# Attention pairs beside the head group of their own number, the last group in a written order, and a gate's modulation summed at the front

## The chip, the cores and the metric

The kernel runs on one core of a Trainium2 chip, in one launch. The metric is device microseconds. The core's engines are TensorE (PE; its weight loads are PEld), VectorE (DVE), ScalarE (ACT), GpSimd (POOL) and SyncE (SP), which here only issues transfers. Each engine works through its own instructions in order and waits on semaphores for the others. A trace's profiled execution is one run of its own.

## The reference

A backbone of two layers works on 512 latent tokens x and 256 context tokens, 1024 wide, in float32; the output is the latent stream.

```python
for i in range(DEPTH):
    mx = jnp.split((cond_x @ ada_w[i] + ada_b[i])[:, None, :], 6, axis=-1)
    mc = jnp.split((cond_c @ ada_w[i] + ada_b[i])[None, None, :], 6, axis=-1)
    ux = modulate(hx, mx[0], mx[1])
    uc = modulate(hc, mc[0], mc[1])
    if i % 2 == 0:
        ox, oc = hybrid_mixer(ux, uc, ...)
    else:
        ox, oc = diff_mixer(ux, uc, ...)
    hx = layer_norm(ALPHA * hx + mx[2] * ox, ln1_g[i], ln1_b[i])
    fx = conv_ffn(modulate(hx, mx[3], mx[4]), ...)
    hx = layer_norm(ALPHA * hx + mx[5] * fx, ln2_g[i], ln2_b[i])
    if not last:
        # the same for hc with mc
```

Layer 0 is the hybrid. One input projection gives z, xbc, dt, q, k and v. The SSD branch (16 heads in 4 groups) works in chunks of 128 tokens: states per chunk, a scan over them in both directions, `y_diag = (C B^T * decay) x` and `y_off = C prev`, then `y * silu(z)` and an RMS norm. Beside it stand 8 heads of neighbourhood attention, whose softmax takes a window of the grid and all context keys; the context attends to itself. `concat(y, a) @ w_out` ends the mixer. Layer 1 has differential attention. Each layer has an FFN with a convolution over three tokens. `mx[5]`, `mc[5]` of layer 0, the gate of its FFN, is called (0, 5) here, or the second gate.

## The kernel before

Matrix products are done in three passes: weights and activations are split into a high half (`whi`, a rounded copy made on ACT) and a low half (`wlo`, the difference, made on DVE or POOL in `wchunk`, L152 to L176), and `PASS` multiplies high by high, high by low and low by high. Tokens lie in six tiles of 128, four of x and two of the context.

The modulation needs a product of the two condition vectors with 1024 x 6144 weights per layer. `ada_steps` (L190) does it on PE. `ada_dve` (L208) does it on DVE: it loads 512 KB at a time (`araw`, two slots under the tag `ar`, shared with `grow` and `yr`), adds up each row times the condition's value in `acc` (L221, L223; for two conditions 32 instructions of 128x512 for one of the six vectors), and lets PE sum over partitions (`adaps`, L229). These pieces are a background list, of which the FFN takes steps.

The hybrid layer, until about 675 us, has at the front the first modulations and the modulated input, the projections of group 0 (`dense_ssd`, `dense_z`, `x_rows`), and then four SSD groups. `ssd_group(g)` transposes B (`btp`), makes the five states (`xw` on POOL, `Sps` on PE, the scan `PV` on POOL and DVE), and then takes six chunks: load the decay rows (`E`, a transfer on POOL's queue from `scr`), eight exponentials on ACT, four pairs of products on DVE (L684, L685), `gp` = B C^T on PE and its product with the decay (L688), `op` = C times the state before it (L695, `t` at L697), `gp` again for the product with x (L706), then the gate with silu(z). `na_pair(p)` splits q and k of a head pair into halves (`split_qk`, `nQ` at L750, `nKh`, `nKl`), transposes V (`vtp`), and takes six units of 128 queries: scores `S` on PE, bias, maximum `nm`, exponential and normalised `P` on DVE and ACT (L799 to L802), transposes of P on PE and their copy `Pt`, and the product with V.

`run` takes a step of the group and of a pair in turn and a step of a list of filler at each second turn; the framework then sets the order of instructions on every engine by a simulated timeline and a priority. While `pe.chain` is True, every matmul through `pe` is tied behind the one before it in the written order. Group g runs beside pair g-1, with the projections of group g+1 and of pair g as filler. In group 3, the filler is pair 3's projection and `early`: it transposes the gated y (`ytp`) and starts two banks of `w_out` (`po`, with 18 matmuls for the six first of eight rows of 128). Pair 3 comes after the group: gate rows `G` are loaded and summed (L291), q and k are split, and its units stand in turn with a `piece` of `w_out`. Then come the other banks, their evacuation (`ev` on DVE, the addition to y on POOL), the last two rows (`out_y2`), the attention's part (`out_att`) and the layer norm.

In the FFN of layer 0, `up(j)` makes two projections (`fpx` for x, `fpc` for the context), with the convolution `cv` on ACT and DVE (L1077, L1081). POOL makes the low half of chunks 4 to 9 (`W_POOL`), and the layer norm's `affine` (L409, `y<-y,gb` on POOL) is tied behind the first of these. `STEPS0` takes five background steps after each of the two up-projections of the second pair, and the first two pieces are the second gate (0, 5) itself.

Of the kernel before, what the change touches and what calls it, by code (L numbers as in the profile page):

```python
# [46 lines left out]
STEPS0 = 5  # L47

ADA_LATER = 100

W_POOL = ((4, 5, 6, 7, 8, 9), (4, 6, 8))
# [23 lines left out]
def emit(tc, T):  # L75
# [74 lines left out]
    pool_wlo = [None]  # L150

    def wchunk(src, shape, gate=None, eng=None, rows=None, rp=None):  # L152
# [55 lines left out]
    def ada_dve(l, w, h, accp, pool, pstag, **atag):  # L208
# [18 lines left out]
        for s in range(ns):  # L227
            for j in range(4):
                nc.tensor.matmul(ps[32 * j:32 * j + 32, 128 * s:128 * s + 128], ones[:, 0:32], acc[:, s, 128 * j:128 * j + 128],  # L229
                                 start=True, stop=True)  # L230
# [52 lines left out]
    def gate_rows(l, which, s, pool, tag, bufs=None, scaled=True):  # L283
# [4 lines left out]
        G = pool.tile([128, D], F32, name="G", tag=tag, bufs=bufs)  # L288
# [50 lines left out]
    def tc_mm(ps, w, u, tt):  # L339
        n = len(PASS) * KC  # L340
        i = 0
        for kc in range(KC):
            for wi, ui in PASS:
                nc.tensor.matmul(ps, u_dst(u, kc, ui, tt), w(kc, wi), start=(i == 0), stop=(i == n - 1))  # L344
                i += 1
# [249 lines left out]
    def dense_z(g):  # L595
        w = by_kc(wrows(T["w_z"][g], 2, (4, 256)), 4)
        for t2 in range(3):
            pz = pmm.tile([128, 2, 256], F32, name="pz", tag="mm")
            zt = sp.tile([128, 2, 256], F32, name="zs", tag="zs", bufs=3)
            for i in range(2):  # L600
                tc_mm(pz[:, i], w, u, 2 * t2 + i)
            nc.scalar.activation(zt, pz, AF.Silu)
# [19 lines left out]
    def ssd_group(g, BC, xs):  # L622
# [37 lines left out]
        for k in range(5):  # L660
# [4 lines left out]
            nc.tensor.matmul(p[:, 0], Bt[:, FO[k]], xw[FO[k]][:, 0].rearrange("p h q -> p (h q)"), start=True, stop=True)  # L665
            nc.tensor.matmul(p[:, 1], Bt[:, BO[k]], xw[BO[k]][:, 1].rearrange("p h q -> p (h q)"), start=True, stop=True)
# [7 lines left out]
        for c in (4, 5, 0, 1, 2, 3):  # L674
# [891 lines left out]
```

## Time and profile before

| | |
|---|---|
| median of 3 runs | 2028.44 us (2028.31 to 2029.06) |
| profiled execution | 2025.07 us, of which the span is 2023.3 |
| mean granted clock of PE | 0.978 |
| PE busy | 1920.8 us, 95% of the span |
| DVE, ACT, POOL busy | 1352.1, 920.5, 769.6 us |
| moved by DMA | 217.59 MB, mean 108 GB/s |

The span runs from the first instruction to the last one. A busy PE may be a slow PE: the granted clock is shown beside it, 1.00 for 2.4 GHz and 0.50 for 1.2 GHz. Waits name the instruction that ended them by line and tile.

### The profile page before, as it was taken

To read this page: it belongs to the slowest core of one execution; us is meant where nothing else is said; L and a number is where in the kernel's file an instruction comes from. 1 tells how busy PE (TensorE), PEld (TensorE's weight loads), DVE (VectorE), ACT (ScalarE), POOL (GpSimd) and SP (SyncE) were. 2 spreads that over 40 slices of the span, in tenths; PEclk is the share of its full clock that TensorE was granted. 3 is DMA by queue.
4 is the path that set the end of the run, shared out by engine and by line. 5 is a ranking of instruction groups with operands and counts; after the bars stand their busy time and mean duration, and the time that the engine had idled before them with its cause. 6 is when DMAs were issued, how large, how long until landed. Compare 5 with 4: busy or idle time off the path is not lost.

```text
span 2023.3 us, 31146 instructions
## 1 busy us (share of the span) xinstructions
PE 1920.8 (95%) x11928; PEld 1645.3 (81%) x11928; DVE 1352.1 (67%) x2172; ACT 920.5 (45%) x1799; POOL 769.6 (38%) x658
## 2 busy tenths in 40 slices
PE   7998999998699889999999999899999899999997
PEld 5887889887477788878888888899998788888886
DVE  3757565765556887887676667566665876655566
ACT  3545466585442732323222234656665644333332
POOL 2135224336315675444444408431115264222133
PEclk9999999999699989999999999999999999999999
DMA  9335342233422243433343342222122223323321
GB/s 314 113 114 170 110 129 76 96 117 117 155 68 88 87 135 100 130 116 115 105 144 106 104 135 86 92 73 85 55 66 68 89 64 126 104 84 104 103 96 62
DMA packets 109445, 217.59 MB, mean 108 GB/s; under 512 B 27112, under 2 KB 45904, under 8 KB 109296
## 3 DMA queue, kind: packets, MB, share of 16 engines
q1 hardware_dynamic: 95168, 187.87, 28.9%
q0 software_dynamic: 6016, 20.03, 2.8%
q10 hardware_dynamic: 8112, 7.71, 1.3%
q8 instruction: 94, 1.54, 0.3%
q14 instruction: 55, 0.45, 0.1%
HBM read 202.81 MB, written 8.55 MB: 104 GB/s over the span
## 4 chain that ended last, share of the span: by engine, by line
PE 72%; DVE 12%; DMA 4%; POOL 4%; ACT 4%; issue 3%; ACTq 0%; SPq 0%; DVEq 0%; POOLq 0%
PE fpx L328 20%; PE pdn L1122 11%; PE px L328 7%; PE fpc L328 5%; PE S L108 3%; PE po L108 3%; PE pc L328 3%; PE pz L344 3%; DVE acc L223 2%; PE pv L344 2%; DMA araw<-in_ada_w 2%; POOL y L409 2%; PE dSp L1329 2%; PE po L1005 2%; PE pk L328 2%
## 5 line engine op out<-in xcount | busy, mean ns | idle before, releaser
L172 ACT ACTIVATE whi<-raw 128x1024 fp32r<-128x1024 f32 (+1 forms) x203 | 213.4, 1056 | 443.5 <-PE fpc L328 167.2
L173 DVE TENSOR_TENSOR wlo<-raw,whi 128x1024 fp32r<-128x1024 f32 (+1 forms) x190 | 251.8, 1330 | 157.4 <-ACT whi L172 144.6
L352 POOL TENSOR_TENSOR y<-y,ev 128x512 f32<-128x512 f32 x144 | 212.5, 1495 | 185.1 <-DVE ev L350 175.2
L1122 PE MATMUL pdn<-whi,fact 128*128 128x512 f32 x880 | 273.1, 392 | 2.1 <-DVE ev L350 1.8
L328 PE MATMUL fpx<-ux,whi 128*128 128x512 f32 (+1 forms) x832 | 232.3, 363 | 8.2 <-DVE cv L1081 7.6
L328 PE MATMUL fpx<-u,whi 128*128 128x512 f32 (+1 forms) x832 | 226.5, 358 | 2.4 <-DVE cv L1081 1.5
L1122 PEld LDWEIGHTS pdn<-whi,fact 128*128 128x128 f32 x880 | 162.4, 188 | 37.2 <-DVE ev L350 2.9
L328 PEld LDWEIGHTS fpx<-ux,whi 128*128 128x128 f32 x832 | 150.3, 194 | 31.1 <-ACT whi L172 8.0
L1122 PE MATMUL pdn<-wlo,fact 128*128 128x512 f32 x440 | 170.8, 390 | 0.7 <-DVE wlo L173 0.7
L328 PEld LDWEIGHTS fpx<-u,whi 128*128 128x128 f32 x832 | 149.2, 191 | 25.1 <-ACT cv L1077 1.6
L328 PE MATMUL fpx<-ux,wlo 128*128 128x512 f32 (+1 forms) x416 | 151.1, 364 | 8.5 <-POOL wlo L173 6.6
L223 DVE SCALAR_TENSOR_TENSOR acc<-araw,condp,acc 128x512 f32<-128x512 f32 x140 | 137.4, 1002 | 24.4 <-DMA araw<-in_ada_w 24.0
L1106 POOL TENSOR_TENSOR fact<-cv,fact 128x768 fp32r<-128x768 f32 (+1 forms) x44 | 70.6, 1605 | 217.5 <-ACT fact L1105 217.5
L328 PE MATMUL fpx<-u,wlo 128*128 128x512 f32 (+1 forms) x416 | 148.8, 358 | 1.1 <-DVE wlo L173 1.1
L328 PE MATMUL px<-ux,whi 128*128 128x512 f32 x448 | 148.5, 405 | 0.0
L171 POOL TENSOR_TENSOR raw<-raw,G 128x1024 f32<-128x1024 f32 x30 | 74.4, 2482 | 193.0 <-DMA raw<-in_w_down 113.0
L1081 DVE SCALAR_TENSOR_TENSOR cv<-fpx,fcw,cv 128x511 f32<-128x511 f32 x176 | 130.3, 744 | 20.8 <-ACT cv L1077 19.6
L328 PE MATMUL fpc<-uc,whi 128*128 128x256 f32 x704 | 130.2, 283 | 0.0
L328 PEld LDWEIGHTS fpc<-uc,whi 128*128 128x128 f32 x704 | 112.6, 191 | 4.2 <-issue 0.6
L409 POOL TENSOR_TENSOR y<-y,gb 128x256 f32<-128x256 f32 x112 | 98.9, 918 | 35.2 <-PE lntp L388 28.7
L1077 ACT ACTIVATE cv<-fpx,fcw 128x512 f32<-128x512 f32 x88 | 67.8, 771 | 80.7 <-PE fpx L328 76.5
L350 DVE SCALAR_TENSOR_TENSOR ev<-pdn,G 128x512 f32<-128x512 f32 x120 | 81.3, 683 | 32.0 <-POOL y L352 18.9
(335 smaller groups left out, 4628.0 us busy)
## 6 DMA issues: line engine op xcount, KB each, us to landing
araw<-in_ada_w SPq DMA_DIRECT2D x96, 512.0 KB
raw<-in_w_up SPq DMA_DIRECT2D x88, 512.0 KB
raw<-in_w_down SPq DMA_DIRECT2D x44, 512.0 KB
E<-scr POOLq DMA_DIRECT2D x24, 512.0 KB, 5.4
raw<-in_w_dqk SPq DMA_DIRECT2D x16, 512.0 KB
raw<-in_w_qkv SPq DMA_DIRECT2D x12, 512.0 KB
raw<-in_w_out SPq DMA_DIRECT2D x12, 512.0 KB
raw<-in_w_bc SPq DMA_DIRECT2D x8, 512.0 KB
```

The costliest lines, as they stand in the source:

```text
L108: i = f(*a, **k)
L171: nc.gpsimd.tensor_tensor(raw, raw, gate, op=OP.mult)
L172: nc.scalar.activation(hi[:, :n], raw[:, :n], AF.Copy)
L173: i = (eng or nc.vector).tensor_tensor(lo[:, :n], raw[:, :n], hi[:, :n].bitcast(F32), op=OP.subtract)
L223: nc.vector.scalar_tensor_tensor(acc[:, s], raw[:, i], cs, acc[:, s], op0=OP.mult, op1=OP.add)
L328: nc.tensor.matmul(ps, w[wi][:, kc], rhs(kc, ui), start=(i == 0), stop=(i == n - 1))
L344: nc.tensor.matmul(ps, u_dst(u, kc, ui, tt), w(kc, wi), start=(i == 0), stop=(i == n - 1))
L350: nc.vector.scalar_tensor_tensor(t, ps, r, Gh, op0=OP.mult, op1=OP.mult)
L352: eng.tensor_tensor(yh, yh, t, op=OP.add)
L409: i = nc.gpsimd.tensor_tensor(y[:, c:c + 256], y[:, c:c + 256], t[:, c:c + 256], op=op)
L1081: nc.vector.scalar_tensor_tensor(dst[:, lo:hi_], src[:, lo + d:hi_ + d], f[:, tap:tap + 1], dst[:, lo:hi_], op0=OP.mult, op1=OP.add)
L1122: nc.tensor.matmul(ps, acts[2 * gs[0] + kt][:, ui, 128 * tt:128 * tt + 128], ws[kt][wi][:, 0, o:o + 512], start=(m == 0), stop=(m == 3 * n ...
```

## The change

Four things change together.

1. The second gate (0, 5) is summed in the front of the hybrid layer. `ada_dve` takes a queue, and its eight loads of 512 KB go through POOL's; `acc` lies in the pool `blk`. The FFN's list of pieces loses (0, 5), `STEPS0` goes (two steps after every up-projection), and `ada_dve`'s matmuls on PE take both conditions in one instruction.
2. Pair g runs beside group g: its projection is one group earlier, and pair 0's lies in the front. q, k and v share one tile. `dense_z` takes the context's tiles first and yields once more per tile.
3. Group 3 is written out in 18 iterations with `pe.chain` True: a step of `early`, up to one of the unit and one of the group. `early` holds `ytp`, the second part of group 3's z projection and half 0 of `w_out` in pieces of nine or six matmuls; four banks are copied to SBUF by ACT and two stay in PSUM. In group 3, the decay of a chunk (`decay`) is made one chunk ahead. After the group come the gate rows, the evacuation, half 1, `out_y2` and `out_att` in the token order 4, 5, 0, 1, 2, 3.
4. In layer 0, POOL makes the low half of chunks 8 to 11 in place of 4 to 9, and `affine` is tied to nothing.

```diff
-STEPS0 = 5
-W_POOL = ((4, 5, 6, 7, 8, 9), (4, 6, 8))
+W_POOL = ((8, 9, 10, 11), (4, 6, 8))
...
+    def ada_dve(l, w, h, accp, pool, pstag, queue=None, **atag):
...
+            (queue or nc.sync).dma_start(raw, src[:, k2:k2 + 2, 1024 * w + 512 * h:1024 * w + 512 * h + 512])
...
+        for j in range(4):
+            nc.tensor.matmul(ps[32 * j:32 * j + 32, 0:128 * ns].rearrange("p (s c) -> p s c", s=ns), ones[:, 0:32],
+                             acc[:, 0:ns, 128 * j:128 * j + 128], start=True, stop=True)
...
-        for c in (4, 5, 0, 1, 2, 3):
+        def decay(c):
...
+            return M
+
+        ready = {FO[0]: decay(FO[0])} if g == 3 else {}
+        for j, c in enumerate(FO):
+            M = ready.pop(c, None)
+            if M is None:
+                M = decay(c)
...
+            if g == 3:
+                yield
+                if j < 5:
+                    ready[FO[j + 1]] = decay(FO[j + 1])
...
-    for _ in chain(dense_ssd(0), dense_z(0), x_rows(0)):
+
+    gate2 = chain(*[ada_dve(0, 5, h, blk, pmm, "mm", nc.gpsimd, tag="b") for h in range(2)])
+    for i, _ in enumerate(chain(dense_ssd(0), dense_na(0), x_rows(0), dense_z(0))):
+        if i > 0:
+            next(gate2, None)
+    for _ in gate2:
         pass
...
+    def mm_y(ps, w, tt, k0, k1):
+        for kt in range(k0, k1):
+            for m, (wi, ui) in enumerate(PASS):
+                pe.matmul(ps, acts[tt][ui][:, kt], w[kt // 2][wi][:, kt % 2], start=(kt + m == 0), stop=(kt == 5 and m == 2))
...
+        for i, tt in enumerate(LAST[:4]):
+            ps = bank()
+            for k0 in (0, 3):
+                mm_y(ps, w0, tt, k0, k0 + 3)
+                if not k0:
+                    yield
+            raw = kept[:, 512 * i:512 * i + 512]
+            nc.scalar.copy(raw, ps)
+            pend.append((tt, 0, raw))
...
+    for g in range(3):
+        fl = [dense_ssd(g + 1), x_rows(g + 1), dense_na(g + 1)]
+        if g < 2:
             fl.append(dense_z(g + 1))
+        run([ssd_group(g, *rows[g]), na_pair(g, *densen[g], [PNA])], chain(*fl))
...
+    pe.chain = True
+    ssd = ssd_group(3, *rows[3])
+    next(ssd)
+    QK3 = split_qk(*densen[3][:2])
+    V3 = na_values(densen[3][2])
+    fl = early()
+    un = None
+    for i in range(18):
+        next(fl, None)
+        if un is not None and i % 3 != 1:
+            next(un, None)
+        next(ssd, None)
+        if i == 0:
+            w0 = w_y(0)
+        if i % 3 == 0:
+            un = na_one(3, i // 3, QK3, V3, na_bias(3, i // 3, np_, 2) if i < 12 else None, PNA, np_, 2, True)
+            next(un)
...
+    for tt in LAST:
         load_res(tt)
     evac_y()
+    w1 = w_y(1)
+    for i, tt in enumerate(LAST):
+        ps = bank()
+        mm_y(ps, w1, tt, 0, 6)
+        pend.append((tt, 1, ps))
+        evac_y()
...
                 up(2 * gi + i, 2 if gi < 2 else 1)
-                if gi == 1 and i == 0 and with_ctx:
-                    for tt in range(3):
-                        affine(Y[tt], gb, pool_wlo[0] if tt == 0 else None)
-                bgstep(STEPS0 if gi == 1 else 2)
+                if gi == 1 and with_ctx:
+                    for tt in range(3 * i, 3 * i + 3):
+                        affine(Y[tt], gb)
+                bgstep(2)
...
-                      [(l, w, h) for l, w in ((0, 5), (1, 0), (1, 1), (1, 2), (1, 4), (1, 3), (1, 5)) for h in range(2)], then)
+                      [(l, w, h) for l, w in ((1, 0), (1, 1), (1, 2), (1, 4), (1, 3), (1, 5)) for h in range(2)], then)
```

On PE, where the last group and pair 3 meet, the rows before are these; `po` is the output projection, `S` a unit's scores, transposes (`c_consts`, the identity) and products with V.

```order
L108 MATMUL po<-wlo,act_5661 128x512
L108 MATMUL S<-c_consts,P 128x128
L108 MATMUL S<-c_consts,P 64x128
L108 MATMUL S<-c_consts,P 128x128 x3
L108 MATMUL S<-c_consts,P 64x128
L108 MATMUL S<-c_consts,P 128x128 x2
L108 MATMUL S<-Pt,V 64x128 x8
L108 MATMUL S<-nKh_4855,nQ_4858 128x256
L108 MATMUL S<-nKl,nQ_4857 128x256
L108 MATMUL S<-nKl,nQ_4858 128x256
L108 MATMUL S<-nKh_4854,nQ_4857 128x256
L108 MATMUL S<-c_consts,P 128x128 x4
```

In the changed order PE's rows inside the last group are these, from the products of one chunk (`gp` and `op`) to the unit's product with V.

```order
L106 MATMUL gp<-xc 128x128
L106 MATMUL op<-PV,xc 128x256
L106 MATMUL po<-whi,act_5335 128x512
L106 MATMUL po<-whi,act_5336 128x512
L106 MATMUL po<-wlo,act_5335 128x512
L106 MATMUL po<-whi,act_5335 128x512
L106 MATMUL po<-whi,act_5336 128x512
L106 MATMUL po<-wlo,act_5335 128x512
L106 MATMUL po<-whi,act_5335 128x512
L106 MATMUL po<-whi,act_5336 128x512
L106 MATMUL po<-wlo,act_5335 128x512
L106 MATMUL S<-Pt,V 64x128 x8
```

Before, the last units of pair 2 stood one behind the other with nothing between their steps; now the steps of pair 3's units and of the group's chunks have nine `po` matmuls between them. The last unit of pair 2 now stands ahead of the group's transposes, like this:

```order
L106 MATMUL pz<-wlo,uc 128x256
L106 MATMUL S<-Pt,V 64x128 x4
L106 MATMUL S<-nKh_4157,nQ_4160 128x256
L106 MATMUL S<-nKh_4158,nQ_4161 128x256
L106 MATMUL S<-nKl,nQ_4160 128x256
L106 MATMUL S<-nKl,nQ_4161 128x256
L106 MATMUL S<-c_consts,P 128x128 x4
L106 MATMUL S<-Pt,V 64x128 x4
L612 MATMUL xtp<-c_consts,xt 128x128 x12
L106 MATMUL vtp<-c_consts,qkv 128x128 x5
```

Between its scores, its transposes and its product with V there is no other row. On DVE, at the start of the FFN, the sums `acc` of the background pieces stood like this among the convolutions `cv`:

```order
L221 TENSOR_SCALAR acc<-araw,condp 128x512 x2
L223 SCALAR_TENSOR_TENSOR acc<-araw,condp,acc 128x512 x3
L1081 SCALAR_TENSOR_TENSOR cv_7164<-fpc,fcw,cv_7164 128x255
L223 SCALAR_TENSOR_TENSOR acc<-araw,condp,acc 128x512 x2
L1081 SCALAR_TENSOR_TENSOR cv_7342<-fpc,fcw,cv_7342 128x255
L1081 SCALAR_TENSOR_TENSOR cv_7164<-fpc,fcw,cv_7164 128x255
L223 SCALAR_TENSOR_TENSOR acc<-araw,condp,acc 128x512
L1081 SCALAR_TENSOR_TENSOR cv_7342<-fpc,fcw,cv_7342 128x255
L223 SCALAR_TENSOR_TENSOR acc<-araw,condp,acc 128x512 x8
L1081 SCALAR_TENSOR_TENSOR cv_7250<-fpc,fcw,cv_7250 128x255 x2
L221 TENSOR_SCALAR acc<-araw,condp 128x512
L1081 SCALAR_TENSOR_TENSOR cv_7428<-fpc,fcw,cv_7428 128x255
```

And they stand like this in the changed kernel, where `G` is the first gate row of the FFN.

```order
L216 TENSOR_SCALAR acc<-araw,condp 128x512 x2
L218 SCALAR_TENSOR_TENSOR acc<-araw,condp,acc 128x512 x6
L1085 SCALAR_TENSOR_TENSOR cv_7228<-fpc,fcw,cv_7228 128x255 x2
L218 SCALAR_TENSOR_TENSOR acc<-araw,condp,acc 128x512 x8
L286 TENSOR_TENSOR G<-G,grow 128x512 x2
L170 TENSOR_TENSOR wlo<-raw,whi 128x1024
L1085 SCALAR_TENSOR_TENSOR cv_7314<-fpc,fcw,cv_7314 128x255
L1085 SCALAR_TENSOR_TENSOR cv_7406<-fpx,fcw,cv_7406 128x511
L1085 SCALAR_TENSOR_TENSOR cv_7314<-fpc,fcw,cv_7314 128x255
L170 TENSOR_TENSOR wlo<-raw,whi 128x1024
L1085 SCALAR_TENSOR_TENSOR cv_7406<-fpx,fcw,cv_7406 128x511
L1085 SCALAR_TENSOR_TENSOR cv_7406<-fpc,fcw,cv_7406 128x255
```

The 32 sums of the gate are gone, 16 of the next piece stand in one block, and the remaining convolutions of the second pair of projections (`cv_7314`, `cv_7406`) stand behind it, two additions to `G` and a `wlo`. On POOL's queue, behind the modulated context `uc`, the front stood like this:

```order
L455 TENSOR_TENSOR uc<-xraw,uc 128x256 x2
L556 DMA scr<-aT 4x6x128 x8
L640 TENSOR_TENSOR xw<-xs,wst 128x512 x4
L700 TENSOR_TENSOR xD<-xs,dsum 128x256 x2
L640 TENSOR_TENSOR xw<-xs,wst 128x512
L671 TENSOR_TENSOR PV<-PV,cdk 128x512
```

Now the gate's loads stand among these rows (two more of them stand ahead of the first `uc`).

```order
L450 TENSOR_TENSOR uc<-xraw,uc 128x256 x2
L209 DMA araw<-in_ada_w 128x2x512 x3
L704 TENSOR_TENSOR xD<-xs,dsum 128x256 x2
L209 DMA araw<-in_ada_w 128x2x512
L765 TENSOR_TENSOR nKl<-qkv,nKh_1460 64x768
L765 TENSOR_TENSOR nKl<-qkv,nKh_1459 64x768
L637 TENSOR_TENSOR xw<-xs,wst 128x512 x4
L209 DMA araw<-in_ada_w 128x2x512
L551 DMA scr<-aT 4x6x128 x8
L209 DMA araw<-in_ada_w 128x2x512
L668 TENSOR_TENSOR PV<-PV,cdk 128x512
```

The loads are issued by POOL in this order, so `nKl` and `xw` stand behind six of them, `scr` behind seven and `PV` behind eight. On SP's queue the end of the first modulations (`araw` of 128x4x256) and the inputs `xraw` stood like this:

```order
L249 DMA araw<-in_ada_w 128x4x256
L447 DMA xraw<-in_xT 128x1024
L125 DMA c_nwc<-in_nwc 128x8
L447 DMA xraw<-in_cT 128x512
L162 DMA raw<-in_w_x 128x1024
L190 DMA araw<-in_ada_w 128x2x512 x2
```

And now like this:

```order
L243 DMA araw<-in_ada_w 128x4x256
L123 DMA c_nwc<-in_nwc 128x8
L159 DMA raw<-in_w_x 128x1024
L159 DMA raw<-in_w_qkv 128x1024
L243 DMA araw<-in_ada_w 128x4x256
L442 DMA xraw<-in_xT 128x1024
L442 DMA xraw<-in_cT 128x512
```

The weights of the x projection and of pair 0's first projection have moved ahead of the last modulation load and of both inputs.

## Rows read from the trace of the kernel before

**Rows 1.** The profile's page: span, busy time of each engine, and its 40 slices.

```profile
span 2023.3 us, 31146 instructions
PE 1920.8 (95%) x11928; PEld 1645.3 (81%) x11928; DVE 1352.1 (67%) x2172; ACT 920.5 (45%) x1799; POOL 769.6 (38%) x658
...
PE   7998999998699889999999999899999899999997
...
PEclk9999999999699989999999999999999999999999
```

**Rows 2.** Stages: length, busy PE, PEld, DVE, ACT, POOL, clock, DMA, GB/s.

```profile
0.00:50.00 50.00, 36.65 (x623) 26.27 (x624) 15.30 (x41) 15.26 (x28) 11.49 (x18) 1.00 0.92 318
50.00:440.00 390.00, 379.22 (x2770) 328.41 (x2769) 255.81 (x549) 232.64 (x494) 134.28 (x173) 1.00 0.37 117
...
480.00:560.00 80.00, 56.38 (x278) 40.54 (x272) 49.78 (x110) 45.43 (x131) 37.54 (x43) 0.72 0.44 147
...
675.00:750.00 75.00, 59.23 (x461) 58.14 (x462) 65.33 (x78) 34.15 (x67) 61.31 (x56) 0.89 0.40 128
```

**Rows 3.** The same table in stretches of 10 us, from 500 to 560.

```profile
500.00:510.00 10.00, 6.31 (x33) 4.72 (x30) 7.68 (x17) 8.98 (x30) 7.79 (x10) 0.75 0.27 85
510.00:520.00 10.00, 9.11 (x39) 6.84 (x39) 6.25 (x16) 4.64 (x12) 4.45 (x6) 0.50 0.60 155
...
540.00:550.00 10.00, 4.47 (x19) 2.90 (x19) 8.21 (x11) 5.96 (x12) 5.09 (x3) 0.50 0.07 21
550.00:560.00 10.00, 5.50 (x19) 2.99 (x19) 6.07 (x12) 4.21 (x16) 2.37 (x2) 0.50 0.18 59
```

**Rows 4.** Waits of PE from 440 to 560: us in total, times, longest.

```profile
PE S L108 <- DVE P L802: 11.7, 3, 9.3
PE gp L706 <- DVE E L688: 4.1, 2, 2.3
PE gp L687 <- DVE t L697: 1.9, 1, 1.9
PE op L695 <- DVE t L697: 1.5, 1, 1.5
```

**Rows 5.** The chain of waits from 440 to 660: start, us, what.

```profile
545.00 2.10 DVE G L291
...
547.44 1.88 DVE G L291
549.34 1.90 DVE nQ L750
551.28 1.91 DVE nQ L750
...
602.38 4.10 PE po L108 x18
```

**Rows 6.** Waits of PE from 690 to 750: us in total, times, longest.

```profile
PE fpx L328 <- DVE cv L1081: 7.6, 2, 7.1
PE fpx L328 <- POOL wlo L173: 6.6, 1, 6.6
```

**Rows 7.** Timeline of POOL and DVE: start, us, instruction, idle before, releaser.

```profile
679.67 24.63 POOL L409 TENSOR_TENSOR y<-y,gb 128x256 f32<-128x256 f32 x28 [4.56 <-ACT ux L401]
...
712.35 10.64 DVE L223 SCALAR_TENSOR_TENSOR acc<-araw,condp,acc 128x512 f32<-128x512 f32 x8 [2.52 <-DMA araw<-in_ada_w]
...
733.26 3.94 DVE L223 SCALAR_TENSOR_TENSOR acc<-araw,condp,acc 128x512 f32<-128x512 f32 x2 [4.10 <-DMA araw<-in_ada_w]
...
817.35 5.03 DVE L223 SCALAR_TENSOR_TENSOR acc<-araw,condp,acc 128x512 f32<-128x512 f32 x6 [0.96 <-DMA araw<-in_ada_w]
```

**Rows 8.** DMA from 0 to 50, in 40 slices.

```profile
GB/s 0 46 324 366 381 335 80 149 369 412 423 397 381 359 347 349 354 379 403 385 361 356 351 350 372 381 365 357 352 312 283 389 380 215 356 359 388 398 134 0
DMA packets 12453, 15.88 MB, mean 318 GB/s; under 512 B 1824, under 2 KB 10144, under 8 KB 12448
```

**Rows 9.** Waits of SP's queue, 0 to 200: us in total, times, longest.

```profile
SPq L190 <- PE adaps L193: 26.2, 8, 7.6
```

More of the change, by code (lines that the diff above doesn't have):

```diff
@@ L281, in fold_ln, with gate_rows @@
             nc.vector.tensor_tensor(sc[:, s], sc[:, s], g, op=OP.mult)
-    def gate_rows(l, which, s, pool, tag, bufs=None, scaled=True):
+    def gate_rows(l, which, s, pool, tag, bufs=None, scaled=True, G=None):
         w = 3 * which + 2
@@ L596, in dense_z @@
         w = by_kc(wrows(T["w_z"][g], 2, (4, 256)), 4)
-        for t2 in range(3):
+        for t2 in (2, 0, 1):
             pz = pmm.tile([128, 2, 256], F32, name="pz", tag="mm")
@@ L734, in dense_na @@
             yield
-        fill()
+        if p:
+            fill()
         densen[p] = q, k, v
@@ L855, in na_pair, with run @@
             yield
-    def run(gens, filler, lower=0):
+    def run(gens, filler):
         filler = iter(filler)
@@ L916, in evac_y @@
             evac(Yt[tt], ps, G[0 if tt < 4 else 1], hf, op4, None, nc.gpsimd, rr[:, tt:tt + 1])
[L918 removed]
     def early():
[L921 to L922 removed]
+        for tt in (4, 5):
             prep_y(tt, 0, 6)
+        for _ in z3:
             yield
[L925 to L944 removed]
@@ new lines, in early @@
+        two = [bank() for _ in range(2)]
+        for k0 in (0, 2, 4):
+            for ps, tt in zip(two, LAST[4:]):
+                mm_y(ps, w0, tt, k0, k0 + 2)
+                yield
+        pend[:0] = [(tt, 0, ps) for ps, tt in zip(two, LAST[4:])]
+    for g in range(3):
+        fl = [dense_ssd(g + 1), x_rows(g + 1), dense_na(g + 1)]
+        if g < 2:
+            fl.append(dense_z(g + 1))
+        run([ssd_group(g, *rows[g]), na_pair(g, *densen[g], [PNA])], chain(*fl))
+    z3 = dense_z(3)
@@ new lines, in emit @@
+    pr = tc.cur_priority
+    tc.cur_priority = pr + 4000
+    for _ in range(2):
+        next(z3)
+    tc.cur_priority = pr
+    pe.chain = True
[15 more added lines that the diff above has]
+            next(un)
@@ L947, in emit @@
+    next(fl, None)
+    next(un, None)
+    for _ in chain(fl, ssd):
+        pass
+    pmm.seq = MM + [(pm3, "mm"), PNA, PNA]
     while bg:
         fill()
-    ssr = sp.tile([128, 6], F32, name="ssr")
-    nc.vector.tensor_reduce(ssr, ssq, axis=AX, op=OP.add)
-    nc.vector.tensor_scalar(ssr, ssr, 1.0 / D, RMS_EPS, op0=OP.mult, op1=OP.add)
-    nc.vector.tensor_scalar(rr, rsqrt_(ssr, sp), 1.0 / ALPHA, None, op0=OP.mult)
     s1.close()
@@ L984, in out_y2 @@
             w = wchunk(T["w_out"][hf, 3], (2, 512), rows=nwc[:, 6:8])
-            for tt in range(6):
+            for tt in LAST:
                 ps = pmm.tile([128, 512], F32, name="po", tag="mm")
@@ L1186, in ffn @@
             if gi < NG - 2:
-                if gi == 1 and with_ctx:
-                    for tt in range(3, 6):
-                        affine(Y[tt], gb)
                 down([gi - 1])
```

149 lines of the change are left out of this document (40 added, 109 removed).

## The prediction

> **What bounds the kernel now.** I read the page's busy times and its 40 slices first, then the table of busy time by stage, then the waits of TensorE (PE) in the two stages that stand out, the chain of waits there, and last the VectorE (DVE) rows behind one of these waits. PE is busy for 1920.8 of 2023.3 us [rows 1]; of its busy digits the lowest between the first slice and the last is the 6 of slice 11, with an 8 before it and two in 14 and 15, and the granted clock's digit is below 9 in slices 11 and 15 alone. So the kernel is bound by PE, and what an edit of order can win is what PE doesn't do in three places. In the table by stage [rows 2] PE's idle time, span less busy, is 13.4 us in 0 to 50, 10.8 in the 390 us of the four groups, 23.6 in 480 to 560 and 15.8 in 675 to 750. In 480 to 560 the mean granted clock is 0.72; taking that mean for the busy part, 56.38 x 0.28 = 15.8 us more go to the lower of the two levels (0.50 is 1.2 GHz of 2.4). In 675 to 750 the same sum is 59.23 x 0.11 = 6.5 us. What can be had at most is therefore about 39 us in the first place, which I call the seam, and 22 us in the second, the start of the FFN. In the slices of the seam [rows 3] PE was busy for 6.31 of the 10 us from 500 at a granted clock of 0.75, then for 9.11 at 0.50, and for 4.47 and 5.50 at 0.50 from 540: the low clock stands behind idle time.
>
> **The work.** The edit leaves almost none out. 80 small matmuls that sum the modulation over partitions become 56, 32 of them as they were and 24 twice as wide; four copies from PSUM on ScalarE (ACT) are new; the low halves of two weight chunks go from GpSimd (POOL) to DVE; eight loads of 512 KB go from SP's queue to POOL's, and with them 32 multiply-adds on DVE from the FFN to the front. On PE that is under 2 us of 1920.8. The sum below is of waits.
>
> **The seam, removed.** PE's waits in 440 to 560 [rows 4]: 11.7 us for the softmax product P, 9.3 of them in one wait, and 4.1 + 1.9 + 1.5 = 7.5 for the SSD chunk steps (decay E, scaled part t). The chain inside that long wait [rows 5] shows what DVE did instead of the softmax: two additions of gate rows to G, 2.10 and 1.88 us, and two splits nQ, 1.90 and 1.91, together 7.8 us that stood ahead of it on DVE. The changed order has neither there: G comes after the group, and pair 3 is split before its first iteration. So the 9.3 goes, to within its own softmax of some 1.5 us. The 7.5 goes because the decay of a chunk is made one chunk ahead. Each step of PE now has nine po matmuls behind it, and 18 of them took 4.10 us [rows 5], 2.05 for nine, against a mean of 4.1 / 2 = 2.05 for the two waits on E. One piece therefore covers one such wait and no more. 9.3 + 7.5 = 16.8 us are removed.
>
> **The seam, late next.** Pair 2 now ends beside group 2, and its last unit stands on PE with nothing between its scores, its transposes and its products with V: two waits, on P and on its transposed copy. The waits on P were 11.7 / 3 = 3.9 us in the mean [rows 4]; 7.8 is the upper end for the two, 0 the lower (the next rows were late anyway), and I take 5, since without the 9.3 the mean of the others is far lower, 1.2. Idle time is then 23.6 - 16.8 + 5 = 11.8 us. The part lost to the clock I scale with the idle time, since the two go together in rows 3: 15.8 x 11.8 / 23.6 = 7.9. The seam then loses 19.7 in place of 39.4: **-20 us**. One end is that all but 1 or 2 us go, -38; the other is worked out as a rival below, +24. I stay in the middle, by the count of waits.
>
> **The start of the FFN.** Two waits make 13.7 of 15.8 us: 7.1 for a convolution cv that stood on DVE behind gate sums, and 6.6 for a low half wlo that POOL made [rows 6]. DVE had eight multiply-adds of 10.64 us, then waited 4.10 us for the next load, then two of 3.94 [rows 7]. The change takes 32 of the sums out and gives POOL chunks 8 to 11 in place of 4 to 9, so both waits lose their cause. But with two steps per up-projection there are still 16 sums in a block ahead of cv, on DVE, and with them two adds to G and a wlo that was POOL's. 16 x 0.84 (5.03 / 6, with POOL idle) are 13.4 us, 16 x 1.33 (10.64 / 8, beside POOL's 24.63 us of additions) are 21.3 [rows 7]. Those additions stay there, ready at the same time. A block of 13 to 21 us against PE's 13.7 us of idle: one wait of some 8 us replaces two. **-5 us**, between -15 and +2 (the whole block beyond what PE has in hand).
>
> The Trainium skill says, in "SBUF — State Buffer", Who interferes with whom, that a DVE instruction with two SBUF inputs contends with a GpSimd instruction that reads SBUF. Rows 7 agree, 1.33 against 0.84 us for the same shape. By that rule alone, with POOL busy throughout, the term would be its +2 end.
>
> **The front.** In 0 to 50 DMA is 0.92 busy [rows 2], at 318 GB/s in the mean and about 370 in most slices [rows 8]. The first two gate loads stand at the head of POOL's queue and so in that stretch: 1.05 MB / 0.37 = 2.8 us. On SP's queue w_x and a w_qkv chunk, 1.05 MB, now go ahead of the last modulation weights and of xT and cT, up to another 2.8. **+4 us**, between 0 (the front's end waits for SP's other loads anyway) and 6. The 32 sums cost DVE 32 x 0.84 = 27 us. It is busy for 15.30 of the first 50 us and 255.81 of the next 390 [rows 2], so there is room, and PE has the new projection of pair 0 beside them: I take nothing, and if that cover is gone, up to 2.1, the mean wait of PE on E, for each of the two gate halves.
>
> The skill's "DMA: Bandwidth & Descriptors", Issuing engines are not separate DMA queues, says that loads from POOL's queue run on the same 16 DMA engines as SP's and interleave with them. Rows 8 can't contradict it. By it a separate queue hides nothing while the engines are full, and the term would be its upper end, 6.
>
> **Behind the gate loads on POOL.** A load waits until its slot, one of two, is free, and POOL's further work stands behind it: nKl of pair 0, xw and scr, which group 0 needs for its states and decays. SP had such waits in 0 to 200, 26.2 us in eight, 7.6 at most [rows 9]. The last two of the eight stand between xw and PV, one of them ahead of scr: 0 to 2 x 7.6 = 15 us, and 26.2 / 8 = 3.3, one mean wait, is what I take, since PE has filler then: **+3 us**.
>
> **The sum.** -20 - 5 + 4 + 3 = -18 against the profiled execution: 2025.07 - 18 = 2007. The runs' median, 2028.44, lies 3.4 above that execution, so **2010 us** as a median.
>
> **Rivals.** *Nearly all goes.* Seam -38, FFN -10, front +4, queue 0: -44, 1984. For it: the dense order gives PE something behind every step. Against it: the po pieces are only as long as the waits.
> *The stall only moves.* DVE is busy for 49.78 of the seam's 80 us, and ACT for 45.43 [rows 2]; the same softmaxes and decays stand in the new order and ACT gets four copies more. If the waits fall between the pieces in other places, the seam stays at 39 and the rest is -5 + 4 + 3: 2030, no change.
> *Slower.* In the last group every PE row is tied in the written order, so a late decay or softmax stops the filler with it. There are twelve such places (six units, six chunks). The five waits of rows 4 on P and E had a mean of (11.7 + 4.1) / 5 = 3.2 us. Were each place to wait that long, the idle time would be 38, and with the clock's part in the old ratio, 38 x 15.8 / 23.6 = 25, the seam would lose 63 in place of 39: +24, and with +2 from the rest 2054. It decides from a seam loss of some 38 us on, 23 us of idle. For it: from 540 to 560 PE was at 1.2 GHz and still idle for half of the time [rows 3]. Against it: before, the decay was made where it was needed, and now it is ahead.
>
> **How the numbers follow.** Forecast 0.52, nearly all gone 0.16, only moved 0.15, slower 0.17. The likeliest's own range, from half a gain at the seam to its better end with the front's and the queue's ends, is 1997 to 2022. The range that holds 8 in 10 takes in most of the second case, the third, and the near part of the fourth: 1988 to 2037. About 0.2%, 4 us, is what a measurement of this kernel can tell from no change. Faster takes the forecast and the second case: 0.68. Within 0.2% is most of the third: 0.13. Slower is the fourth and a little of the third: 0.19.
>
> **What would show it.** At the seam: no DVE addition to G and no nQ split between two softmaxes; PE idle of about 12 us in the stretch that ends with the w_out pieces, the longest wait under 5 us, and a mean granted clock above 0.85. At the start of the FFN: no wait for a wlo from POOL, one wait for cv behind 16 sums. In the front: PE's first projection later by 3 to 6 us. The forecast is wrong if the last group has idle time of over 23 us in waits on P, E or M, or if group 0 waits for scr or xw behind POOL's loads for over 10 us.

## The result, and the profile after

The changed kernel takes 2040.35 us (median of 4 runs, 2036.92 to 2042.37) against 2028.68 (4 runs) of the kernel before: 1.006 times, with an interval of 1.0045 to 1.0076. It is slower by 12 us where 18 less were forecast, and outside the range.

Where the time went is read from three points of the two traces: the first projection of the front (`px`), the first of the FFN (`fpx`) and the first of layer 1 (`pv`). The rows are the changed kernel's:

```profile
22.24 1.05 PE L323 MATMUL px<-ux,whi 128*128 128x512 f32 x2
...
687.61 0.74 PE L323 MATMUL fpx<-ux,whi 128*128 128x256 f32 x4 [0.62 <-ACT whi L169]
...
1266.76 0.96 PE L106 MATMUL pv<-wv,ux 128*128 128x256 f32 x6
```

| | px | fpx | pv | end of the span |
|---|---|---|---|---|
| before | 19.96 | 675.24 | 1260.39 | 2023.3 |
| after | 22.24 | 687.61 | 1266.76 | 2035.1 |
| after later by | 2.3 | 12.4 | 6.4 | 11.8 |

So the front begins 2.3 us later, the rest of the hybrid layer loses 10 more, the FFN gains 6.0, and layer 1, whose code is the same, takes 5.4 more in this execution. The busy times by stage answer to [rows 2]; the last row is a stage of the kernel before that is not among those.

```profile
0.00:50.00 50.00, 34.27 (x579) 24.21 (x580) 14.45 (x37) 15.26 (x27) 13.12 (x20) 1.00 0.93 317
50.00:440.00 390.00, 376.59 (x2732) 317.56 (x2732) 263.23 (x536) 224.13 (x469) 119.85 (x148) 0.99 0.37 119
...
480.00:560.00 80.00, 65.20 (x421) 54.13 (x419) 37.85 (x79) 50.20 (x118) 37.18 (x43) 0.87 0.30 96
560.00:675.00 115.00, 100.19 (x473) 80.13 (x472) 83.94 (x157) 45.04 (x123) 59.02 (x57) 0.94 0.37 125
675.00:750.00 75.00, 65.39 (x479) 62.58 (x477) 65.51 (x95) 42.87 (x93) 55.55 (x53) 0.95 0.37 120
...
560.00:675.00 115.00, 114.47 (x582) 90.16 (x580) 74.28 (x147) 50.23 (x124) 43.82 (x36) 0.99 0.22 71
```

PE's idle time is 15.7 us in the first 50 us (13.4 before), 13.4 in the groups (10.8), and 14.8 + 14.8 from 480 to 675 (23.6 + 0.5). In these two stages the granted clock is 0.87 and 0.94, so 65.2 x 0.13 + 100.19 x 0.06 = 14.5 us go to the lower level, 15.8 + 1.1 before. The seam's loss is no smaller, 29.6 + 14.5 = 44.1 us against 24.1 + 16.9 = 41.0; before, nearly all of it lay in the first of the two stages, and now it is spread over both. The waits there, which answer to [rows 4]:

```profile
PE ytp L106 <- DMA yr<-scrY: 7.0, 1, 7.0
PE S L106 <- DVE nm L814: 6.0, 1, 6.0
PE S L106 <- ACT att L846: 6.0, 2, 5.0
PE gp L106 <- DVE E L692: 3.7, 1, 3.7
PE S L106 <- ACT Pt L801: 2.1, 3, 1.0
PE po L106 <- DVE ev L345: 2.0, 1, 2.0
PE po L106 <- ACT yr L913: 1.9, 1, 1.9
```

Four of them can be followed on the engines behind them. At the end of group 2 stands the wait of 6.0 us, in pair 2's last unit. DVE took its maximum, then pair 3's two splits (4.19 us), and only then the reciprocal; ACT had five casts of the same split before the exponential.

```profile
489.45 0.76 DVE L812 TENSOR_REDUCE nm<-S 128x1 f32<-128x256 f32 x2
490.24 4.19 DVE L763 TENSOR_TENSOR nQ<-qkv,nQ 64x768 fp32r<-64x768 f32 x2
494.48 0.16 DVE L814 RECIPROCAL nm<-nm 128x1 f32<-128x1 f32 x1
...
495.17 1.12 PE L106 MATMUL S<-c_consts,P 128*128 128x128 f32 x4 [6.03 <-DVE nm L814]
```

The next, 5.05 us, is a unit's second score matrix. It needs the PSUM bank of the unit before, and ACT's copy out of it (`att`) stands behind the exponentials of two chunks, high halves of w_out and the silu of z.

```profile
518.45 2.45 ACT L678 ACTIVATE E<-E,acs 128x128 f32<-128x128 f32 x8
...
522.03 2.43 ACT L678 ACTIVATE E<-E,acs 128x128 f32<-128x128 f32 x8
...
525.77 0.60 ACT L599 ACTIVATE zs<-pz 128x512 f32<-128x512 f32 x1
...
527.49 0.25 ACT L846 COPY att<-S 128x128 f32<-128x128 f32 x1
...
527.80 0.80 PE L106 MATMUL S<-nKh,nQ 128*128 128x512 f32 x1 [5.05 <-ACT att L846]
```

The wait of 3.7 us is again for the decay. The last, 6.95 us, is for a load of y, which on SP's queue waits for a slot that a gate row holds; DVE could sum the gate rows only when both had landed, at 602. The gate row's own load left SP's queue only at 597.9: it had waited there for a transfer of the group's gated y out of `xD`.

```profile
SPq L284 <- DMA scrY<-xD: 3.1, 1, 3.1
...
601.98 1.29 DVE L286 TENSOR_TENSOR G<-G,grow 128x512 f32<-128x512 f32 x2 [5.74 <-DMA G<-in_ada_br]
...
606.26 0.66 PE L106 MATMUL ytp<-c_consts,yr 128*128 128x128 f32 x2 [6.95 <-DMA yr<-scrY]
```

In the front two things are new. In the first 60 us PE's wait for the loads of the first modulations, which go through SP's queue, is longer; the first of the next rows is the changed kernel's, the second that of the kernel before.

```profile
PE adaps L246 <- DMA araw<-in_ada_w: 12.2, 4, 5.8
...
PE adaps L252 <- DMA araw<-in_ada_w: 8.9, 4, 5.6
```

And DVE is full: 20.00 of 20 us from 60 to 80, as the next rows show (columns as in rows 2, then as in rows 7). Eight sums of the gate, 5.3 us, stand between convolutions, and PE waits 3.8 us for a convolution behind them.

```profile
60.00:80.00 20.00, 14.76 (x107) 12.46 (x107) 20.00 (x33) 7.73 (x12) 0.00 (x0) 0.93 0.52 174
...
59.68 0.88 DVE L216 TENSOR_SCALAR acc<-araw,condp 128x512 f32<-128x512 f32 x2
60.47 1.41 DVE L218 SCALAR_TENSOR_TENSOR acc<-araw,condp,acc 128x512 f32<-128x512 f32 x2
61.80 0.74 DVE L561 SCALAR_TENSOR_TENSOR xc<-px,c_scw,xc 128x510 f32<-128x510 f32 x1
...
68.60 0.74 DVE L218 SCALAR_TENSOR_TENSOR acc<-araw,condp,acc 128x512 f32<-128x512 f32 x1
...
76.12 1.10 PE L188 MATMUL adaps<-araw,condp 128*32 128x128 f32 x32 [3.80 <-DVE xc L561]
```

At the start of the FFN the waits that answer to [rows 6] are these.

```profile
PE fpx L323 <- DVE cv L1085: 3.9, 1, 3.9
PE fpx L323 <- DVE wlo L170: 3.3, 1, 3.3
PE fpc L323 <- DVE cv L1085: 1.8, 1, 1.8
```

### The profile page after: what moved, and what is told of

It reads as the page before. It is cut to its first block, busy times and chain, and to the rows that moved or that the text cites. A ratio compares the mean times of both kernels' runs of the same rounds, so it can differ in the third digit from the quotient of the medians.

```text
span 2035.1 us, 31082 instructions
## 1 busy us (share of the span) xinstructions
PE 1925.0 (95%) x11880; PEld 1646.9 (81%) x11880; DVE 1360.7 (67%) x2169; ACT 924.8 (45%) x1810; POOL 781.0 (38%) x664
## 5 line engine op out<-in xcount | busy, mean ns | idle before, releaser
L170 DVE TENSOR_TENSOR wlo<-raw,whi 128x1024 fp32r<-128x1024 f32 (+1 forms) x192 | 259.5, 1357 | 171.0 <-ACT whi L169 155.4
L218 DVE SCALAR_TENSOR_TENSOR acc<-araw,condp,acc 128x512 f32<-128x512 f32 x140 | 130.1, 954 | 25.7 <-DMA araw<-in_ada_w 24.9
L404 POOL TENSOR_TENSOR y<-y,gb 128x256 f32<-128x256 f32 x112 | 106.6, 987 | 34.2 <-PE lntp L383 30.4
L323 PE MATMUL fpc<-uc,wlo 128*128 128x256 f32 x352 | 100.4, 285 | 0.0
```

Of the source, the lines that this page charges most:

```text
L218: nc.vector.scalar_tensor_tensor(acc[:, s], raw[:, i], cs, acc[:, s], op0=OP.mult, op1=OP.add)
L323: nc.tensor.matmul(ps, w[wi][:, kc], rhs(kc, ui), start=(i == 0), stop=(i == n - 1))
L404: i = nc.gpsimd.tensor_tensor(y[:, c:c + 256], y[:, c:c + 256], t[:, c:c + 256], op=op)
```

## Experiments

All times are medians, ratios are to the kernel before on the same chip. Kernels with no gate part have (0, 5) in the FFN. The first fpx is read from one execution, the profiled one, which lies up to 7.4 us from its kernel's median, so a few us between two of them are not a result by themselves.

| kernel | us | ratio, interval | first fpx |
|---|---|---|---|
| changed | 2040.35 | 1.0060 (1.0045 to 1.0076) | 687.6 |
| gate part alone | 2069.00 | 1.0198 (1.0185 to 1.0211) | 711.2 |
| no gate part | 2033.12 | 1.0028 (1.0018 to 1.0037) | 679.9 |
| split behind | 2034.94 | 1.0039 (1.0026 to 1.0051) | 687.0 |
| y later | 2046.03 | 1.0097 (1.0083 to 1.0111) | 705.4 |
| gate in groups | 2048.47 | 1.0103 (1.0083 to 1.0123) | 695.4 |
| gate on SP's queue | 2041.05 | 1.0065 (1.0042 to 1.0087) | 693.1 |
| yr in its own slots | 2039.80 | 1.0058 (1.0038 to 1.0078) | 691.9 |
| three mends | 2046.57 | 1.0095 (1.0071 to 1.0120) | 700.6 |
| narrow sums | 2021.77 | 0.9974 (0.9964 to 0.9985) | 675.5 |
| no gate, free order | 2021.86 | 0.9973 (0.9964 to 0.9982) | 666.5 |
| no gate, split | 2029.51 | 1.0000 (0.9988 to 1.0012) | 678.3 |
| no gate, decay in place | 2031.51 | 1.0016 (1.0004 to 1.0028) | 678.2 |
| free order | 2032.61 | 1.0029 (1.0018 to 1.0040) | 689.6 |
| no gate, free, split | 2037.81 | 1.0058 (1.0044 to 1.0072) | 675.5 |

**One part at a time.** The gate part alone, on the kernel before:

```diff
-    for _ in chain(dense_ssd(0), dense_z(0), x_rows(0)):
+    gate2 = chain(*[ada_dve(0, 5, h, blk, pmm, "mm", nc.gpsimd, tag="b") for h in range(2)])
+    for i, _ in enumerate(chain(dense_ssd(0), dense_z(0), x_rows(0))):
+        if i > 0:
+            next(gate2, None)
+    for _ in gate2:
         pass
...
-STEPS0 = 5
+STEPS0 = 2
```

> The kernel before with the gate part alone: gate (0, 5) summed in the front with its loads on POOL's queue, two background steps after each up-projection; pairs, last group and W_POOL as before. Theory 1 (the loss of 12 us is made of a later front, +6, and of waits in the last group that only moved, +6, while the start of the FFN gains 6): front +3 to +4 without the second projection there, start of the FFN -6, so 2026 (2022 to 2031). Theory 2 (the gate's loads are the whole loss): 2040. Theory 3 (the whole loss is the order of pairs and of the last group, the gate only gains): 2022 or less.

It was slower by 40 us, outside all three. And the changed kernel without this part:

```diff
-    gate2 = chain(*[ada_dve(0, 5, h, blk, pmm, "mm", nc.gpsimd, tag="b") for h in range(2)])
...
+    for _ in chain(dense_ssd(0), dense_na(0), x_rows(0), dense_z(0)):
         pass
...
-                bgstep(2)
+                bgstep(5 if gi == 1 else 2)
```

> The changed kernel without its gate part: no gate sums in the front, (0, 5) back at the head of the FFN's pieces with five steps after each of the second pair's up-projections; all of the rest as changed. Theory 1: front -4, start of the FFN +6, so 2042 (2037 to 2047). Theory 2: 2028. Theory 3: 2046 to 2050.

2033 lies between the theories: about half of the loss is the gate part, and about half the rest of the change. The gate part beside the new order costs 7 us by the medians, though the FFN gains 6 by it (fpx to pv takes 585.5 us without it and 579.2 with it): that makes some 13 us in the hybrid layer, of which the two traces show 7.7 at the first fpx. In the old order it costs far more, and the FFN gains nothing by it (589.3 us from fpx to pv, 585.2 before). From 60 to 130 PE is busy for 57.8 us there, for 62.0 in the changed kernel and for 66.8 without the gate part. That the old order has no projection of pair 0 in the front may be a reason, but it is not shown, and the 4 us between the first two are a small part of the 36 by which the first fpx is late there. The rows are the gate part alone, then no gate part:

```profile
60.00:130.00 70.00, 57.82 (x450) 50.37 (x448) 57.30 (x108) 30.88 (x44) 17.21 (x21) 0.93 0.43 135
...
60.00:130.00 70.00, 66.75 (x490) 59.22 (x490) 40.93 (x78) 32.13 (x49) 14.04 (x16) 0.95 0.30 95
```

**Single waits.** Pair 3's split tied behind pair 2's last unit:

```diff
+            if late:
+                for i in (a, b, c):
+                    behind(i, ends["act"])
+                behind(d, ends["dve"])
```

> The changed kernel with the split of pair 3's q and k tied behind the last unit of pair 2 (its casts on ACT behind that unit's copy of the output, its subtractions on DVE behind that unit's P). Theory 1: PE's wait of 6.0 us in that unit falls to about 1.5, with some clock 2034 to 2036. Rival (the next wait in the written order, 5.1 us for ACT's copy of a unit's output, takes it up): 2039 to 2041, and that wait grows to 8 or more.

The wait on `nm` fell from 6.0 to 2.2 and the kernel gained 5 us, though the first fpx only 0.6: that this wait falls is shown, and the wait for `att` didn't grow (3.9 us in two), but where the runs gain the 5 us isn't.

```profile
PE S L106 <- DVE nm L821: 2.2, 1, 2.2
```

The transposes of the last rows of y, two banks later:

```diff
-        prep_y(tt, 6, 2)
+        if i > 1:
+            prep_y(LAST[i - 2], 6, 2)
...
```

> The changed kernel with the transposes of the last two rows of y (and their loads) two banks later in half 1. Theory 1: PE's wait of 7.0 us for a load of y goes, as two more banks of 18 matmuls stand ahead of it, -6 to -8, so 2032 to 2035. Rival (PE then waits for the evacuation, since G comes late and a bank is missing): the wait changes its name to ev, 2038 to 2041.

It was slower still, outside both: the wait on the load stayed, 6.0 us in two, and one on the evacuation came on top. The transposes take their banks from the ring that `po` uses.

```profile
PE ytp L106 <- DVE ev L345: 6.3, 1, 6.3
PE ytp L106 <- DMA yr<-scrY: 6.0, 2, 5.4
```

Slots of their own for these loads:

```diff
+        if k0:
+            yr = np_.tile([128, 512], F32, name="P", tag="P", bufs=2)[:, :128 * kn]
```

> The changed kernel with the loads of the last two rows of y (yr, 128x256) in the slots of the softmax's P, free by then, so that they no longer wait for the slots of the gate rows. Theory 1 (the 7.0 us wait is one for these slots): it falls below 1.5, 2033 to 2036. Rival (PE then waits for the evacuations, which wait for the gate rows G themselves, as happened when the transposes were moved): the wait moves to ev, 2038 to 2042.

The rival was right: the wait on the load is gone, and 7.1 us in two on `ev` stand in its place. What is late there is the sum of the gate rows (DVE waits 5.8 us for their load here too), for which the changed order has no cover left.

```profile
PE po L106 <- DVE ev L345: 7.1, 2, 4.5
```

**Where the gate is summed.** Beside groups 1 and 2:

```diff
+            for _ in gen:
+                next(gate2, None)
+                yield
```

> The changed kernel with the gate's sums not in the front but one step after each step of the filler of groups 1 and 2; queue and all else as changed. Theory 1 (the front is the wrong place: there DVE is full with convolutions and DMA with loads, 60 to 82 us, and POOL's queue carries scr and xw; elsewhere the sums are hidden): the front as without the gate (first px at 19 us), the start of the FFN 6 earlier than without the gate, so 2027 (2024 to 2030). Rival (the sums cost what they cost wherever they stand in the hybrid layer): 2036 to 2042.

My theory fell, and the rival was still too mild. The front was as it should be (the first px at 18.4), but the first fpx came 15.5 us later than without the gate part, against 7.7 with the gate in the front. The sums stand from 254 to 380 there, and from 300 to 400 PE is busy for 88.96 us at 0.91, without the gate part for 99.71 at 1.00. So it was not the front alone that had no room; and full with loads the front was not, DMA's share from 60 to 80 is 0.52 in the changed kernel. And on SP's queue:

```diff
-    gate2 = chain(*[ada_dve(0, 5, h, blk, pmm, "mm", nc.gpsimd, tag="b") for h in range(2)])
+    gate2 = chain(*[ada_dve(0, 5, h, blk, pmm, "mm", nc.sync, tag="b") for h in range(2)])
```

> The changed kernel with the gate's eight loads on SP's queue in place of POOL's. If POOL's queue is what costs (scr, xw and nKl behind loads that wait for a slot): 2033 to 2036. If DVE's crowded stretch and the DMA in the front cost: 2039 to 2044, as the sums stand where they stood.

No change in the time: the queue isn't what costs. The first px is earlier (19.8, and PE's wait for SP's loads is 9.0 us again), but the first fpx is not. The three edits (the split, the own slots and the sums beside the groups) together:

> The changed kernel with three edits together: gate sums beside groups 1 and 2, pair 3's split behind pair 2's last unit, yr in its own slots. Theory 1: the gains add up, -13 for the front, -5 and -5: 2017 to 2022, below the kernel before. Rival (each wait that goes is taken by the next in the written order): 2026 to 2032.

Slower than the change and outside both: its gate part is that of the groups, and the two other edits give nothing beside it. What the sums cost was then taken away by itself:

```diff
+        cw = 1 if (l, w) == (0, 5) else 512
...
-                        nc.vector.scalar_tensor_tensor(acc[:, s], raw[:, i], cs, acc[:, s], op0=OP.mult, op1=OP.add)
+                        nc.vector.scalar_tensor_tensor(acc[:, s, 0:cw], raw[:, i, 0:cw], cs, acc[:, s, 0:cw], op0=OP.mult, op1=OP.add)
```

> The changed kernel with the gate's 30 additions made one column wide in place of 512 (the gate is left out by that; the loads, the slots and the number of instructions stay, so DVE is relieved of some 20 us in the front). If DVE's time is what the gate costs: the front's wait of 3.8 us for a convolution goes and 2027 to 2033, near the kernel without the gate part less its 6 us at the FFN. If the loads (4 MB more in the front, POOL's queue) are what it costs: 2038 to 2042.

By the medians 18.6 us less than the changed kernel and below the kernel before (28 additions are narrow by the trace; four multiplications stay wide). PE's busy time from 60 to 130 rose from 62.0 to 68.2, with the same loads, and PE's 3.8 us wait is gone. So DVE's time for the sums is a cost of the gate part, but 18.6 is not its price: this kernel is also 11 us faster than the one with no gate part at all, of which the FFN's gain explains 6. The scheduler sees cheaper sums and sets other rows elsewhere too. A full DVE alone doesn't stop PE either: from 60 to 80 DVE is busy for 19.52 us in this run, and PE for 18.61. What counts is which rows stand there: the convolution that PE waited 3.8 us for is in time. That the first px stays late (22.6, against 18.9 without the gate part) and the wait for SP's loads long (12.6 us) gives the loads their share, some 3.5 us. The rows are the changed kernel, then the narrow sums:

```profile
60.00:130.00 70.00, 62.01 (x460) 54.04 (x460) 60.69 (x108) 34.49 (x51) 20.29 (x22) 0.98 0.42 134
...
60.00:130.00 70.00, 68.23 (x517) 59.38 (x516) 47.79 (x113) 36.91 (x62) 17.86 (x22) 1.00 0.49 150
```

**The tied order.** Without the gate part, PE's order in group 3 left to the scheduler:

```diff
-    pe.chain = True
     ssd = ssd_group(3, *rows[3])
...
+    pe.chain = True
     pmm.seq = MM + [(pm3, "mm"), PNA, PNA]
```

> The changed kernel without its gate part (2033) and with PE's order in group 3's iterations left to the scheduler; from half 1 on PE is tied as before. If the tied order is what costs (one late softmax or copy stops the filler too): 2025 to 2029, with the 5.1 us wait for ACT's copy and the 3.7 us wait for E gone. Rival (the scheduler's own order puts the filler in the wrong places, since its timeline does not show these waits): 2033 to 2042.

11 us less than with the tied order, and by the ratio 5.5 below the kernel before: the fastest kernel here that computes everything. The wait for E falls from 4.3 us to 0.2 and the one for `att` is halved. From 480 to 560 PE is busy for 70.67 of 80 us at 0.94, where it was 62.83 at 0.88. In the traces the first fpx comes 13.4 us earlier. Not all of that is the seam: its loss, idle and clock from 480 to the first fpx, goes from some 44 to some 38 us, and about 5 are won ahead of 480. From there the FFN takes 3.7 us more and layer 1 5.6 less. So the tie is a cost, and some 6 us of it are seen in its own place. The rows are the tied order's stage without the gate part, then the free order's stage and waits:

```profile
480.00:560.00 80.00, 62.83 (x377) 50.82 (x378) 41.08 (x93) 51.80 (x131) 42.22 (x50) 0.88 0.30 97
...
480.00:560.00 80.00, 70.67 (x425) 57.32 (x424) 50.58 (x117) 58.09 (x144) 43.95 (x54) 0.94 0.36 117
...
PE S L106 <- DVE P L815: 9.8, 4, 6.9
PE ytp L106 <- ACT zs L599: 4.2, 2, 3.5
PE S L106 <- DVE nm L814: 4.1, 2, 2.2
PE ytp L106 <- DMA yr<-scrY: 3.4, 1, 3.4
PE S L106 <- ACT att L846: 2.4, 1, 2.4
```

The split and the decay, without the gate:

> The changed kernel without its gate part and with pair 3's split tied behind pair 2's last unit, as in the earlier run that had the gate part. If the two gains add: 2033 - 5 = 2028 (2026 to 2030), level with the kernel before. Rival (the wait is taken up by the next): 2032 to 2035.

By the ratios the split gains 5.7 us (1.0028 to 1.0000), by the medians, which stand beside different runs of the kernel before, 3.6: the first theory, within its range.

```diff
-        ready = {FO[0]: decay(FO[0])} if g == 3 else {}
+        ready = {}
...
-                if j < 5:
-                    ready[FO[j + 1]] = decay(FO[j + 1])
```

> The changed kernel without its gate part and with the decay of each chunk of group 3 made where it is used, not one chunk ahead. If the decay ahead is a gain (it took away 7.5 us of waits on E and t): these waits are back, 2037 to 2043. If it is a loss (two decays' 16 exponentials stand ahead of ACT's copy of a unit's output, the 5.1 us wait): 2027 to 2031.

Between the two, and inconclusive on `att`: the wait for it is still 5.1 us, because ACT, which nothing ties, makes the same 16 exponentials of two chunks there. The wait on E is 2.9 us in place of 3.7. So the decay ahead buys nothing that can be measured (the intervals overlap).

```profile
PE S L106 <- ACT att L844: 5.1, 1, 5.1
PE gp L106 <- DVE E L692: 2.9, 1, 2.9
```

The free order with the gate, and with the split:

> The changed kernel, gate part and all, with PE's order in group 3's iterations left to the scheduler. If the tied order costs by itself, as it did without the gate part (11 us): 2040 - 11 = 2029 (2026 to 2032), that is level with the kernel before. Rival (the two parts meet: with the gate's sums in the front the scheduler's order in group 3 is another one): 2034 to 2040.

> The changed kernel without its gate part, with PE's order in group 3 left to the scheduler and pair 3's split behind pair 2's last unit. If the split's gain (4 us, twice) adds to that of the free order: 2022 - 4 = 2018 (2015 to 2020), the fastest so far. Rival (the free order puts other rows there already): 2021 to 2024.

With the gate the free order gains 7.7 us by the medians, 6.3 by the ratios, between what the two theories said. Its trace doesn't show it in the hybrid layer (first fpx at 689.6 against 687.6) but in the FFN (573.5 us from fpx to pv against 579.2): the profiled executions are 3.4 us below the median for the changed kernel and at it for this one, so how much of it is the seam stays open. The split behind the last unit, a gain in the tied order, is a loss of 16 us in the free one: the first fpx is 9 us later. Which wait takes it wasn't followed.

## Why the prediction was wrong

**The step that failed** is the seam, -20: "9.3 + 7.5 = 16.8 us are removed", and 5 come new. For the hybrid layer I had -20 + 4 + 3 = -13, and the first fpx came 12.4 us late. The gate part makes 7.7 of these, near the +7 of the front and the queue. The rest of the change makes 4.7 (679.9 without the gate part, 675.2 before) where -20 stood, and that is some 25 of the 30 us by which the sum missed; 5.4 more are in layer 1.

What was to be removed did go in part: no gate row and no split stands between pair 3's softmaxes, and the waits of 7.5 us for the chunk steps became 3.7. The reason given for these doesn't hold: with the decay made where it is used, the wait on E is 2.9. The wait at pair 2's last unit was foreseen with 5 us and measured 6.0; but its cause is the very split that I had counted as removed: it has moved to that unit. Not foreseen were a copy on ACT (6.0 us in two), y's load behind the gate rows (7.0) and smaller ones on ACT and `ev` (6.0 in sum). I had counted the waits that go, and looked for new ones on DVE and PE alone; the new ones are on ACT, on a slot, and on the gate rows that lost the cover of pair 3. Together the waits listed are 28.7 us, against 11.8 of idle time forecast, and the seam lost 44.1 us against 41.0 before. Of the signs named ahead, a clock above 0.85 in the seam came true (0.87), and the longest wait, to stay under 5 us, was 7.0.

So the rival in which the stall only moves describes the seam best: it stayed where it was. The rival on the slower side named a cause that the runs bear out in part: the tied order in the last group costs 11 us without the gate part. Its condition held, 29.6 us of idle against 23 (before, 24.1). But its price, +24, is far above the 3 to 5 us that the seam lost, since twelve places did not all wait, and few of the waits were on P or E. Why the dense order as a whole gains nothing is thus shown only so far: lifting the tie brings back some 6 us at the seam, and the single mends show that a wait there can come back under another name.

**The second** is the price of the 32 sums: "there is room, and PE has the new projection of pair 0 beside them: I take nothing". DVE's mean over the stretch, 15.30 of 50 and 255.81 of 390 us, hid that from 60 to 80 it was already busy for 18.50 of 20 us in the kernel before:

```profile
60.00:80.00 20.00, 19.24 (x171) 17.05 (x171) 18.50 (x32) 9.62 (x12) 0.00 (x0) 1.00 0.50 159
```

The sums filled it, and PE waits there for DVE. The runs put 7 us on the gate part in all, 7.7 (traces) to 13 (medians) in the hybrid layer against its gain in the FFN. That the traces' 7.7 is near my +7 is luck, for more than half of it is a term that I had put at nothing. The +4 for the loads was 3.3: that is the growth of PE's wait for SP's loads, 8.9 to 12.2 us (9.0 without the gate part). The weights that moved ahead of them cost nothing (without the gate part the first px is at 18.9, before at 19.96). The +3 for POOL's queue was nothing: PE has no wait for `scr` or `xw` in group 0 of the changed trace, and with the loads on SP's queue the time is the same. The other 4 us or more are the sums, which I had put at nothing.

**Right** was the start of the FFN: -5 forecast, -6.0 measured, no wait for a `wlo` of POOL, two for `cv` (3.9 and 1.8), and a new one of 3.3 for a `wlo` on DVE. The two edits there gain only together: the new chunks for POOL and the free `affine` without the gate part give 585.5 us from fpx to pv, the gate part alone 589.3, and before it was 585.2. The 16 sums took 1.73 + 6.95 + 9.02 = 17.7 us, within the 13 to 21 forecast. Of rows 7 one reading was wrong: the 24.63 us of additions on POOL end at 704.3, and the eight sums from 712.35 stand beside the next ones of the same kind; the price of 1.33 us is right all the same. The Trainium skill's rule on DVE and GpSimd ("SBUF — State Buffer", Who interferes with whom) would have put that term at its +2 end. The trace agrees with the rule in that eight sums beside POOL's 49.91 us of additions took 9.02 us, 1.13 each against 0.84, but the term did not come to that.

The Trainium skill's rule in "DMA: Bandwidth & Descriptors", Issuing engines are not separate DMA queues, agrees with the front: loads on POOL's queue lengthened the wait for SP's from 8.9 to 12.2 us. On SP's own queue the gate's loads gave 2041.05 us against 2040.35.

Layer 1 takes 5.4 us more in the changed kernel's trace than before, with the same code. It doesn't stand in the rows of the seam or of the gate: over all traces it takes 762 to 770 us, and the time goes with the order that the scheduler gives it. In the two kernels without the gate part and with the free order DVE's rows of layer 1 stand nearly as before (99% match), and it takes 763.3 and 762.3 us, before 762.9. In all others the order is another one (91 to 96% match), and it takes 765.8 to 770.4. Which rows cost it stays open.

## What to carry to other kernels

Room on an engine is to be read in slices as short as the stretch in which the added work will stand, and in the slices where it waits for a neighbour: a mean of 66% hid a stretch of 93%. A wait that is removed from one place is to be looked for on all engines, slots and transfers behind the new place. An order tied by hand is worth trying against the scheduler's before it is tuned: here two of three mends in the tied order came back as other waits, and freeing the order gained more than any mend, though how much of that was won in the freed stretch is seen only in part. Where a scheduler sets the rest, an edit in one place moves rows in others: a difference of a few us is to be looked for stage by stage before it is put down to the edit.

## What was not expected

The gate part costs some 40 us net in the old order, 7 in the new one, and 15 (2048.47 against 2033.12) with the sums beside groups 1 and 2, where I had looked for room. The edits' gains don't add: three mends gave 2046.57, and a split that gains 4 to 6 us in one order costs 16 in another.
